# A hybrid attention/Hyena step: one adaLN chunk moved from TensorE to VectorE

## The chip, the cores and the metric

The kernel runs on one NeuronCore of one Trainium2 chip. The metric is device time in microseconds (us) of one execution. Five engines run in parallel on the core: TensorE (PE in the profile, its weight loads PEld), VectorE (DVE), ScalarE (ACT), GpSimd (POOL) and SyncE (SP, which here only issues DMAs). Each works through its own instructions in the order in which they were issued.

## The reference, cut to what matters

A two-layer diffusion backbone on 384 tokens (256 latent, 128 context), width 2048, everything in 32-bit floats. Per layer:

```python
shift, scale, gate = split(silu(c) @ w_ada[l] + b_ada[l], 3)     # adaLN: one vector for latents, one for context
h    = rmsnorm(x, norm_g) * (1 + scale) + shift
proj = h @ w_in                          # 2048 x 6144: q|k|v|g_att|hyena x0,x1,v|g_hy
att  = attend(q, k_all, v_all) * silu(g_att)
hy   = hyena(x0, x1, v) * silu(g_hy)     # short convolution, then a long one by Fourier transform
x    = x + gate * (concat(att, hy) @ w_out)
```

The adaLN part is a product of two vectors (one for the latents, one for the context) with a 2048 x 6144 matrix in each layer. Its output is cut into 12 chunks of 512 columns: chunks 0 to 3 are the shift, 4 to 7 the scale, 8 to 11 the gate. Chunk (1, 5) is a quarter of the scale of layer 1; it must be there when layer 1 forms its input h, at the end of layer 0.

## The kernel before, in words

The large products run as units. A unit is one 128 x 2048 block of weights, loaded in two halves of 512 KB into seven raw buffers `raw`. Each half is split into a high part `hi` (ACT, L225) and a rest `lo` (DVE, L231), and three matmuls (hi x hi, hi x lo, lo x hi; L831 to L833 or L803 to L805) give the product in nearly full precision. A half's raw buffer is free once its `lo` is made. One pass of the main loop is a step: it multiplies one unit on PE, splits halves of the next two units, evacuates the product and runs waiting background work (attention, the Fourier convolution). Layer 0 has, after a start phase, units of kind "b" (q, k, v; four steps each), 40 units "a" (f = 8 to 15 for x0; 16, 24, 17, 25, ... 23, 31 for x1 and v in turn; 0 to 7 and 32 to 39 for the two gates) and 16 units "o" (the output projection, f = 0 to 15). Layer 1 has the same.

The 16 adaLN chunks that are not needed at the start are spread over these steps. The string `HOW` says how each is made, in the order (0, 8), (0, 9), (0, 10), (0, 11), (1, 4), (1, 0), (1, 5), (1, 1), (1, 6), (1, 2), (1, 7), (1, 3), (1, 8) to (1, 11):

- "P", on PE (`ada_mm`, L283): four units of four small matmuls each (`adab`), then one copy by ACT, four transposes (L297), and two small DVE instructions. `P_0` says in which steps of layer 0 a unit is loaded; it is multiplied one step later, after the unit's matmuls.
- "D", on DVE (`ada_acc`, L357 and L359): 32 multiply-adds over 128 x 512, 16 for each of the two vectors, into two accumulators `pa0` and `pa1`. They wait in a queue `vq`; the lists `R_Q`, `R_X0`, `R_X1`, `R_G`, `R_O` (layer 0) and `R_1` say how many run in each step, at the step's end (`run_q`; up to two that could not run are owed to the next step). A finished chunk is added up over the partitions by PE in the next step (`ada_sum`, four matmuls, L379), copied by ACT (L381) and transposed in the step after that (`ada_fin2`, L387). The next chunk's first multiply-add stays queued until the sum has been issued.
- "G", the gap chunks (1, 3) and (1, 7): their weights are loaded during the output projection of layer 0 into the buffers that attention and convolution have left, and PE multiplies them around the layer boundary, where it waits for the norm. Their results are copied by ACT (L290) into the accumulator buffers `pa0` and `pa1`, of which there is one each (`PAB = 1`).

`load_ada` is called at the end of each step: it loads a unit of a "P" chunk if it is due, and then halves of "D" chunks while fewer multiply-adds are queued than the next two steps want and a raw buffer is free. All these loads go through the SP queue, in the order of the program.

At the layer boundary the last unit of the output projection (f = 15) is evacuated (L879), the norm's sums go over PE (L421), ACT and DVE, and back over PE (L435); ACT copies the result to `rs` (L436). Then `make_h` builds the input of layer 1: DVE scales (L446), ACT adds the shift and rounds (L450, `hh`), DVE takes the rest (L453, `hl`). The matmuls of layer 1 (L803 to L805) need `hh` and `hl`.

Of the kernel before, what the change touches and what calls it, by code (L numbers as in the profile page):

```python
# [29 lines left out]
HIB = 4  # L30
LOB = 3
PAB = 1
HOW = 'PDPDDDPDDDGGDDDD'
SQ = 3
MAINB = 4
AH = 2
# [4 lines left out]
EB = 0.8  # L41
W0, W1, W2, W3, W4 = 6, 8, 4, 24, 0
R_Q = [0, 0, 0, 0, 2, 2, 4, 5]
R_X0 = [5, 6] * 4
R_X1 = [5, 6] * 2 + [5] + [4, 4, 4, 3] + [2, 1, 0, 0, 1, 2, 2]
R_G = [2, 1, 1, 0, 0, 1, 3, 4, 4, 6, 6, 6, 6, 6, 5, 0]
R_O = [3] + [5] * 14 + [0]
R_1 = [0] * 12 + [4] * 21 + [1] * 14 + [6] * 5 + [0] * 20
P_0 = [1] * 6 + [0] * 19 + [1] * 6 + [0] * 33
GAP_L, GAP_P = (0, 1, 3, 7, 8, 9, 11, 12), (5, 6)  # L50
P_1 = [0] * 72
BUD = 2.0
# [18 lines left out]
def step_kernel(ctx, tc, xT, vec, cst, delta, zfeat, fw, ada, wb, wc, wo, ck, cv, qk1, yT, nk, nv):  # L71
# [75 lines left out]
    free = [one.tile([128, 1024], F32, name=f"raw{n}") for n in range(RAWB)]  # L147
# [10 lines left out]
    def fetch(u, h, of=None):  # L158
        u.raw[h] = free.pop(0)
        if of:  # L160
            u.of = of
            held[of] += 1
        nc.sync.dma_start(out=u.raw[h], in_=u.src[:, h * 1024:(h + 1) * 1024])
# [37 lines left out]
    def load_ada(n, p):  # L201

        state["pe"] += p
        if state["pe"] and by_pe and len(free) > 1:
            state["pe"] -= 1
            u = by_pe.pop(0)
            for h in range(2):
                fetch(u, h)
            on_pe.append(u)
        while by_dve and len(vq) < n and free:  # L210
            i, h = divmod(state["ada"], 2)
            u = by_dve[0]
            fetch(u, h)
            ada_acc(u, h)
            state["ada"] += 1
            if h == 1:
                by_dve.pop(0)
# [115 lines left out]
    vq, by_pe, by_dve, on_pe = [], [], [], []  # L333

    def ada_acc(u, h):
        l, ch, kc = u.kw["l"], u.kw["ch"], u.kw["kc"]
        if kc == 0 and h == 0:
            pacc[0] = {"left": 32}
        st = pacc[0]

        def done():
            st["left"] -= 1
            if st["left"] % 4 == 0:
                release(u, h)
            if st["left"] == 0:
                sums.append(lambda: ada_sum(l, ch, st))
                urgent.append((state["step"] + 1, run_sums))

        def op(t, v):
            if v not in st:  # L350
                st[v] = accs_p.tile([128, 512], F32, name=f"pa{v}", tag=f"pa{v}")
            acc = st[v]
            w = u.raw[h][:, t * 512:(t + 1) * 512]
            k = kc * 4 + 2 * h + t
            sc = scT[:, k, v:v + 1]
            if k == 0:
                nc.vector.tensor_scalar(acc, w, sc, None, ALU.mult)  # L357
            else:
                nc.vector.scalar_tensor_tensor(out=acc, in0=w, scalar=sc, in1=acc, op0=ALU.mult, op1=ALU.add)  # L359
            done()  # L360

        for t in range(2):
            for v in range(2):
                vq.append((kc + h + t + v == 0, lambda t=t, v=v: op(t, v)))
# [547 lines left out]
    def ada_units(l, ch, how="P"):  # L912
        return [Unit(ada[l, ch, kc], "ada", l=l, ch=ch, kc=kc, how=how) for kc in range(4)]
# [26 lines left out]
    chunks += [(1, ch) for ch in range(8, 12)]  # L940
    for (l, ch), how in zip(chunks, HOW):
        if how != "G":
# [6 lines left out]
    gap = ada_units(1, 3) + ada_units(1, 7)  # L949
    spare = [p[:, 1024 * i:1024 * (i + 1)] for p, n in ((P1, 3), (P2, 4), (P3, 3), (P4, 2)) for i in range(n)]  # L950
    mains = []
    for l in range(NL):
        us = ([k_unit(1, j) for j in range(4)] if l else []) + layer_units(l)

        for u, n, p in zip(us, R_1 if l else R_Q + R_X0 + R_X1 + R_G + R_O, P_1 if l else P_0):
            u.dq, u.pe = n, p
# [27 lines left out]
    with tc.manual_schedule():  # L984
# [18 lines left out]
        for i, u in enumerate(units + mains):  # L1003
# [28 lines left out]
            l = u.kw["l"]  # L1032
# [72 lines left out]
            if v is not None:  # L1105
                load_ada(v.dq + (v.nxt.dq if v.nxt is not None else 0), v.pe)
# [97 lines left out]
```

## Time and profile before

| | before |
|---|---|
| median of 3 runs | 1493.04 us (1490.0 to 1494.1) |
| the profiled execution: its time | 1492.46 us |
| its span, from first to last instruction | 1490.7 us |
| PE busy | 1461.4 us (98%) |
| DVE busy | 976.7 us (66%) |
| ACT busy | 586.2 us (39%) |
| mean DMA rate | 192 GB/s |
| mean granted PE clock | 0.994 |

Times in the profile's views are us from the start of the span. A row of a timeline gives start, duration, engine, line of the program, operation, output <- inputs, shapes and, in brackets, how long the engine was idle just before it and what ended that. Rows that follow each other closely are merged (x4). A matmul's stated duration includes its way through the array; the distance of the starts of two rows is the time that PE spent on the first. "x8" in a row of small matmuls counts four weight loads and four matmuls.

### The profile page before, as it was taken

The page shows a single profiled execution, that of the slowest core. Times are in us where ns is not written, and L with a number is a line of the kernel's source. Part 1 is how long each engine was busy: PE and PEld are TensorE (multiplying, and loading weights), DVE is VectorE, ACT ScalarE, POOL GpSimd, SP SyncE. Part 2 cuts the span into 40 slices and gives each one's busy share as a digit, 9 for nine tenths or more (in the row PEclk, how much of TensorE's full clock was granted, in tenths as well). Part 3 has the DMA queues.
Part 4 walks back from the last instruction along what each step waited for, and adds up shares of the span by engine and source line. Part 5 has one row for each costly group of instructions (what it writes and reads, how often), then busy time and mean ns, then how long its engine had stood idle before and what let it go on. Part 6 is the DMA issues. An engine that isn't in the chain of part 4 may idle for free.

```text
span 1490.7 us, 20718 instructions
## 1 busy us (share of the span) xinstructions
PE 1461.4 (98%) x8032; PEld 1293.2 (87%) x8032; DVE 976.7 (66%) x1619; ACT 586.2 (39%) x975; POOL 51.1 (3%) x94
## 2 busy tenths in 40 slices
PE   9999999999999999999999999999999999999995
PEld 5346777999998999999997888899999999999995
DVE  6734556777877566697687655766777756755443
ACT  2423554555432322343334545455433332244331
POOL 1110000000000000001110000000000000000001
PEclk9999999999999999999999999999999999999997
DMA  9999366444566543569894333543445343544422
GB/s 349 414 358 346 134 224 224 163 152 155 172 223 215 206 144 132 184 196 327 282 329 152 115 120 135 194 145 128 156 170 184 128 171 128 196 158 149 148 98 85
DMA packets 78731, 286.48 MB, mean 192 GB/s; under 512 B 9670, under 2 KB 10504, under 8 KB 78120
## 3 DMA queue, kind: packets, MB, share of 16 engines
q1 hardware_dynamic: 72824, 267.19, 50.8%
q0 software_dynamic: 5808, 17.97, 3.3%
q8 instruction: 63, 1.03, 0.3%
q14 instruction: 36, 0.29, 0.1%
HBM read 271.49 MB, written 13.63 MB: 191 GB/s over the span
## 4 chain that ended last, share of the span: by engine, by line
PE 91%; DMA 5%; DVE 2%; ACT 1%; issue 1%; SPq 0%; DVEq 0%; ACTq 0%
PE acc L831 21%; PE acc L833 21%; PE acc L832 21%; PE acc L803 6%; PE acc L805 6%; PE acc L804 6%; PE adab L283 2%; PE bgb L665 1%; PE bgb L648 1%; DMA hh1b<-in_ada 1%; DMA hl2b<-in_wb 1%; PE bgb L756 1%; DMA hl1b<-in_ada 1%; DMA XM<-in_xT 1%; PE bgb L658 1%; DMA raw<-in_wb 1%
## 5 line engine op out<-in xcount | busy, mean ns | idle before, releaser
L831 PE MATMUL acc<-hh,hi 128*128 128x384 f32 x1792 | 613.9, 343 | 0.0
L833 PE MATMUL acc<-hh,lo 128*128 128x384 f32 x1792 | 602.7, 336 | 0.0
L832 PE MATMUL acc<-hl,hi 128*128 128x384 f32 x1792 | 602.6, 336 | 0.0
L225 ACT CAST hi<-raw 128x1024 fp32r<-128x1024 f32 x282 | 294.4, 1045 | 318.0 <-issue 168.0
L231 DVE TENSOR_TENSOR lo<-raw,hi 128x1024 fp32r<-128x1024 f32 x282 | 343.0, 1219 | 116.3 <-issue 53.9
L831 PEld LDWEIGHTS acc<-hh,hi 128*128 128x128 f32 x1792 | 337.0, 188 | 12.5 <-issue 8.9
L832 PEld LDWEIGHTS acc<-hl,hi 128*128 128x128 f32 x1792 | 337.0, 188 | 3.7 <-issue 1.4
L833 PEld LDWEIGHTS acc<-hh,lo 128*128 128x128 f32 x1792 | 336.8, 188 | 0.0
L359 DVE SCALAR_TENSOR_TENSOR pa<-raw,scT,pa 128x512 f32<-128x512 f32 x330 | 225.9, 744 | 0.0
L803 PE MATMUL acc<-hi,hh 128*128 128x512 f32 x384 | 156.2, 407 | 4.2 <-ACT hh L450 3.9
L804 PE MATMUL acc<-lo,hh 128*128 128x512 f32 x384 | 152.2, 396 | 0.8 <-DVE lo L231 0.8
L805 PE MATMUL acc<-hi,hl 128*128 128x512 f32 x384 | 152.6, 397 | 0.0
L803 PEld LDWEIGHTS acc<-hi,hh 128*128 128x128 f32 x384 | 72.5, 189 | 37.4 <-issue 13.4
L805 PEld LDWEIGHTS acc<-hi,hl 128*128 128x128 f32 x384 | 72.5, 189 | 18.1 <-DVE hl L453 0.7
L804 PEld LDWEIGHTS acc<-lo,hh 128*128 128x128 f32 x384 | 72.6, 189 | 17.6 <-DVE lo L231 1.5
L406 ACT ACTIVATE tt<-XM 128x384 f32<-128x384 f32 x48 | 24.4, 523 | 135.2 <-DVE XM L879 131.0
L879 DVE SCALAR_TENSOR_TENSOR XM<-acc,mod,xo 128x256 f32<-128x256 f32 x64 | 23.7, 412 | 67.0 <-PE acc L833 67.0
L722 DVE SCALAR_TENSOR_TENSOR z<-acc,V,z 128x255 f32<-128x255 f32 (+1 forms) x64 | 25.2, 414 | 37.5 <-ACT z L718 36.4
L722 DVE SCALAR_TENSOR_TENSOR XM<-acc,V,XM 128x255 f32<-128x255 f32 (+1 forms) x64 | 25.2, 414 | 30.1 <-ACT XM L718 29.0
L283 PE MATMUL adab<-raw,scT 128*32 128x512 f32 x248 | 41.0, 610 | 2.7 <-ACT tt L406 1.5
L722 DVE SCALAR_TENSOR_TENSOR x1c<-acc,V,x1c 128x255 f32<-128x255 f32 (+1 forms) x64 | 25.2, 414 | 26.5 <-ACT x1c L718 25.3
L450 ACT ACTIVATE hh<-tt,mod 128x256 fp32r<-128x256 f32 x64 | 24.7, 446 | 37.5 <-DVE tt L446 37.5
(188 smaller groups left out, 1109.1 us busy)
## 6 DMA issues: line engine op xcount, KB each, us to landing
raw<-in_wc SPq DMA_DIRECT2D x160, 512.0 KB, 3.8
raw<-in_ada SPq DMA_DIRECT2D x150, 512.0 KB, 5.2
raw<-in_wo SPq DMA_DIRECT2D x64, 512.0 KB, 4.4
raw<-in_wb SPq DMA_DIRECT2D x58, 512.0 KB, 4.6
P<-in_ada SPq DMA_DIRECT2D x16, 512.0 KB, 8.0
Hd<-P POOLq DMA_DIRECT2D x24, 256.0 KB, 8.8
P<-Hd SPq DMA_DIRECT2D x4, 1536.0 KB, 8.6
XM<-in_xT SPq DMA_DIRECT2D x4, 768.0 KB, 11.4
```

Source lines behind the costliest of these rows:

```text
L225: nc.scalar.copy(u.hi[h], u.raw[h])
L231: nc.vector.tensor_tensor(u.lo[h], u.raw[h], u.hi[h].bitcast(F32), ALU.subtract)
L283: mm(part[32 * t:32 * t + 32, :], scT[:, kc * 4 + t, :], u.raw[t // 2][:, (t % 2) * 512:(t % 2 + 1) * 512], start=(kc == 0), stop=(kc == 3))
L359: nc.vector.scalar_tensor_tensor(out=acc, in0=w, scalar=sc, in1=acc, op0=ALU.mult, op1=ALU.add)
L450: nc.scalar.activation(hh[:, kt, a:b], t[:, a:b], AF.Identity, bias=mod[l][:, kt, v:v + 1])
L722: nc.vector.scalar_tensor_tensor(out=out[:, o:o + n], in0=bank[:, i:i + n], scalar=w(k), in1=out[:, o:o + n], op0=ALU.mult, op1=ALU.add)
L803: mm(accs[g][m], hh[:, kt, ms], wh[:, k, :], start=first, stop=False)
L804: mm(accs[g][m], hh[:, kt, ms], wl[:, k, :], start=False, stop=False)
L805: mm(accs[g][m], hl[:, kt, ms], wh[:, k, :], start=False, stop=last)
L831: mm(b[:, :T], wh, hh[:, kt, :], start=(kt == 0), stop=False)
L832: mm(b[:, :T], wh, hl[:, kt, :], start=False, stop=False)
L833: mm(b[:, :T], wl, hh[:, kt, :], start=False, stop=(kt == 15))
```

## The change

The seventh letter of `HOW`, chunk (1, 5), turns from P to D. The lists of multiply-adds are raised for it in layer 0, mostly from 5 to 6 per step, `P_0` now loads the eight remaining PE units in the first eight steps, and `load_ada` gets one more condition: no multiply-add of a gate chunk of layer 1 is loaded before the gap chunks are done.

```diff
-HOW = 'PDPDDDPDDDGGDDDD'
+HOW = 'PDPDDDDDDDGGDDDD'
...
-R_X0 = [5, 6] * 4
-R_X1 = [5, 6] * 2 + [5] + [4, 4, 4, 3] + [2, 1, 0, 0, 1, 2, 2]
-R_G = [2, 1, 1, 0, 0, 1, 3, 4, 4, 6, 6, 6, 6, 6, 5, 0]
-R_O = [3] + [5] * 14 + [0]
+R_X0 = [6] * 8
+R_X1 = [6] * 4 + [6] + [5, 5, 5, 5] + [4, 3, 2, 1, 1, 2, 2]
+R_G = [2, 2, 2, 1, 1, 2, 4, 5, 6, 6, 6, 6, 6, 6, 5, 0]
+R_O = [4] + [6] * 14 + [0]
...
-P_0 = [1] * 6 + [0] * 19 + [1] * 6 + [0] * 33
+P_0 = [1] * 8 + [0] * 56
...
-        while by_dve and len(vq) < n and free:
+        while by_dve and len(vq) < n and free and (gap == [] or by_dve[0].kw["ch"] < 8 or by_dve[0].kw["l"] == 0):
```

## The prediction, made before the changed kernel was built or run

> **What bounds the kernel now.** I read the page first: engines and the chain that ended last.
>
> ```profile
> span 1490.7 us, 20718 instructions
> PE 1461.4 (98%) x8032; PEld 1293.2 (87%) x8032; DVE 976.7 (66%) x1619; ACT 586.2 (39%) x975; POOL 51.1 (3%) x94
> PE 91%; DMA 5%; DVE 2%; ACT 1%; issue 1%; SPq 0%; DVEq 0%; ACTq 0%
> ```
>
> PE is busy nearly always, and 91% of the chain is PE. A busy share is a mean over stages, so I then asked for the stretch that the change touches, layer 0 from its first "a" unit to its last "o" unit. Columns: stretch, length, busy time of PE, PEld, DVE, ACT, POOL with instruction counts, granted PE clock, DMA share, GB/s.
>
> ```profile
> 256.00:794.00 538.00, 538.00 (x3127) 512.70 (x3125) 395.26 (x628) 198.67 (x312) 17.36 (x32) 1.00 0.60 206
> ```
>
> PE has no idle microsecond in these 538 us. Here every piece of PE work taken out shortens the time by its own length, and work on DVE costs nothing until PE has to wait for it. DVE is busy 73% of the stretch.
>
> Third, the layer boundary, where PE does wait: timelines of ACT, DVE and PE.
>
> ```profile
> 801.96 0.59 ACT L290 COPY pa<-adab 128x512 f32<-128x512 f32 x1 [4.76 <-PE bgb L379]
> 802.44 0.48 ACT L436 COPY acc<-bgb 128x384 f32<-128x384 f32 x1
> 802.81 1.06 ACT L225 CAST hi<-raw 128x1024 fp32r<-128x1024 f32 x1
> 804.02 0.82 ACT L450 ACTIVATE hh<-tt,mod 128x256 fp32r<-128x256 f32 x2
> ...
> 802.96 0.74 DVE L446 SCALAR_TENSOR_TENSOR tt<-XM,asc,bgb 128x256 f32<-128x256 f32 x2 [3.71 <-ACT acc L436]
> ...
> 797.88 0.91 PE L435 MATMUL bgb<-tt,ones 128*128 128x128 f32 x6
> 798.71 2.78 PE L283 MATMUL adab<-P,scT 128*32 128x512 f32 x24
> 801.31 0.61 PE L379 MATMUL bgb<-pa,ones 128*32 128x256 f32 x8
> 801.74 1.04 PE L283 MATMUL adab<-P,scT 128*32 128x512 f32 x8
> 804.60 0.50 PE L803 MATMUL acc<-hi,hh 128*128 128x512 f32 x1 [1.82 <-ACT hh L450]
> 806.32 0.80 PE L803 MATMUL acc<-hi,hh 128*128 128x512 f32 x1 [0.70 <-ACT hh L450]
> 815.62 0.60 PE L297 MATMUL bgb<-C,pa 128*128 128x128 f32 x4
> 816.19 0.48 PE L803 MATMUL acc<-hi,hh 128*128 128x512 f32 x1
> 824.67 0.60 PE L297 MATMUL bgb<-C,pa 128*128 128x128 f32 x4
> ```
>
> Read it backwards. PE waits at 804.60 for `hh` (ACT L450). ACT is late because it sat idle 4.76 us before its copy L290 into `pa`: with one `pa0`, the gap chunk's result must wait until the sum of the last DVE chunk, (1, 2), has read it, and that sum (L379) stands on PE only at 801.31, behind 2.60 us of gap products. The norm copy L436 could have run when L435 ended at 798.71, but it is queued behind L290; DVE's L446 waits for L436, and everything of layer 1 for that.
>
> **The change, part by part.** First, PE work that goes. The six PE units that stand in steps f = 28, 21, 29, 22, 30, 23, from the chain (start, us, what; x8 is four weight loads and four matmuls), the work around them, and the restart behind them:
>
> ```profile
> 444.75 0.99 PE adab L283 x8
> ...
> 464.79 1.56 PE adab L283 x8
> ...
> 499.01 1.00 PE adab L283 x8
> ...
> 440.55 0.57 PE bgb L379 x8
> ...
> 454.46 0.38 PE L387 MATMUL bgb<-C,tt 128*128 128x128 f32 x2
> 454.77 1.06 PE L283 MATMUL adab<-raw,scT 128*32 128x512 f32 x8
> ...
> 464.19 0.60 PE L297 MATMUL bgb<-C,tt 128*128 128x128 f32 x4
> 464.72 1.63 PE L283 MATMUL adab<-raw,scT 128*32 128x512 f32 x8
> ...
> 445.67 0.45 PE L831 MATMUL acc<-hh,hi 128*128 128x384 f32 x1
> 445.96 0.34 PE L832 MATMUL acc<-hl,hi 128*128 128x384 f32 x1
> 446.14 0.34 PE L833 MATMUL acc<-hh,lo 128*128 128x384 f32 x1
> ```
>
> A unit costs PE about 1.0 us, not four times the 0.6 us of one matmul: the four run side by side. Five units are 0.99 to 1.00, one 1.56; in all 6.5 us. Four of these six are chunk (1, 5); two are the end of (0, 10), which with `P_0 = [1] * 8` come at the end of the "b" units instead: 2.0 us come back there. One set of L297 transposes goes: 464.19 to 464.72, 0.53 us. In their place stands one more sum (L379, 0.57) with its L387 (0.31 by the starts). Moreover the sum of (1, 2) moves from the boundary into a step, another 0.88 there. Each new interruption of a unit's run costs a restart: 0.29 us to the second matmul instead of 0.17 to 0.18, 0.1 us; I count three more. Sum: -6.5 + 2.0 - 0.53 + 2 x 0.88 + 0.3 = -3.0 us. Bounds: -2.4, if the 1.56 was a stall that comes back elsewhere, to -3.6.
>
> Second, the boundary. Does (1, 2) end earlier? Stepping `run_q` and `load_ada` through the lists by hand: before, 224 multiply-adds (seven chunks) are needed in layer 0; 153 have run by the end of step f = 39, and the remaining 71 go 3, 4, 6, five times 5, 1, 7, five times 5: the last runs at f = 14, so its sum falls behind f = 15, where the row at 801.31 shows it. After, 256 are needed; 183 have run by f = 39 and the remaining 73 go 4, 5, 7, 6, 6, 6, 6, 1, 8, 6, 6, 6, 6: the last runs at f = 12, the sum at f = 13, L387 at f = 14. The new condition in `load_ada` keeps the next chunk from taking `pa0` and `pa1`. So L290 finds `pa0` free. Then: L435 ends at 798.7, L436 takes 0.48 (to 799.3; L290, 0.59, is done before), L225 0.95 more (800.2), L450 starts then, and PE may start 0.58 later (804.02 to 804.60), at 800.8. PE itself is through with its gap products at 801.31 + 1.0 = 802.3 without the 0.43 of L379. So PE is late next, not `hh`: it starts at 802.3 instead of 804.6, 2.3 us earlier. The second block of `hh`, 2.30 after the first L450 (806.32), comes at 802.5, before PE needs it at 803.0; its wait goes too. The first unit of layer 1 takes 804.60 to 815.62, 11.0 us; the next 816.19 to 824.67, 8.5. The 2.5 between them is that second wait (0.7 by its row, with the pieces around it about 1) and this:
>
> ```profile
> 806.30:809.50 3.20, 3.18 (x8) 2.53 (x9) 3.20 (x10) 2.22 (x6) 0.00 (x0) 0.50 0.00 0
> ```
>
> The granted clock (third from the end) falls to 0.50 after the two waits: eight matmuls take 3.2 us, against 0.235 each otherwise: 1.4 us lost. Without the waits I take the clock to stay at 1.00, as in the rows before them. Boundary: -2.3 - 2.5 = -4.8 us. Bounds: -0.4 (only L379 gone, ACT waits for something else) and -4.8 (no wait left); I take -4.8, as 4.76 us of wait have one named cause.
>
> The Trainium skill, page "TensorE: Matmul & The Clock Gate", Part 1, says the clock halves after an idle window of about 3.4 us. The gaps here are 1.8 and 0.7 us; by that rule the slow stretch need not come from them and could stay, and the time would be about 1486.5.
>
> Third, DVE. 32 more multiply-adds:
>
> ```profile
> 642.26 4.05 DVE L359 SCALAR_TENSOR_TENSOR pa<-raw,scT,pa 128x512 f32<-128x512 f32 x6
> ...
> 785.95 0.74 DVE L879 SCALAR_TENSOR_TENSOR XM<-acc,mod,xo 128x256 f32<-128x256 f32 x2 [0.84 <-PE acc L833]
> ...
> 788.89 3.39 DVE L359 SCALAR_TENSOR_TENSOR pa<-raw,scT,pa 128x512 f32<-128x512 f32 x5
> ...
> 794.27 0.74 DVE L879 SCALAR_TENSOR_TENSOR XM<-acc,mod,xo 128x256 f32<-128x256 f32 x2 [0.85 <-PE acc L833]
> ```
>
> Six take 4.05 us, so 0.68 each, 22 us in all, hidden by DVE's idle time. In the output projection a step is 8.32 us (785.95 to 794.27); with 5 DVE idles 0.85 of it, with 6 it keeps 0.17: nearly full, not over. The step that runs 8 falls 0.6 behind. What is queued behind the multiply-adds is the `lo` of a later unit's second half, which PE reads half a unit (4.2 us) after the next evacuation; lateness under 4 us is covered. Tightest are the steps of the Fourier products, where PE's step shrinks too. The DVE rows that open them:
>
> ```profile
> 465.09 1.65 DVE L722 SCALAR_TENSOR_TENSOR z<-acc,V,z 128x255 f32<-128x255 f32 x4 [1.50 <-ACT z L718]
> ...
> 475.66 1.64 DVE L722 SCALAR_TENSOR_TENSOR x1c<-acc,V,x1c 128x255 f32<-128x255 f32 x4 [2.16 <-ACT x1c L718]
> ...
> 487.26 1.65 DVE L722 SCALAR_TENSOR_TENSOR z<-acc,V,z 128x255 f32<-128x255 f32 x4 [3.65 <-ACT z L718]
> ```
>
> At f = 21: two more multiply-adds (+1.35), a PE step shorter by 1.3, 0.35 of small DVE work moved away, 1.50 idle: 0.8 us late. At f = 29: 0.8 + 1.35 + 2.1 - 0.35 - 2.16 = 1.7 late. At f = 22 the idle time takes it back. 1.7 is under 4: nothing. Without that cover PE would pay those 1.7.
>
> Loads: bytes stay the same; they move earlier on SP's queue. In the output projection:
>
> ```profile
> raw<-in_ada SPq DMA_DIRECT2D x17, 512.0 KB, 6.2
> DMA to landing us min/median/max: 3.6/5.8/12.1
> ```
>
> A half loaded in one step is used in the next at the earliest, a step (8.4 us) later; the median landing is 6.2. Main loads queue on SP behind an adaLN load that waits for a buffer; its release comes at most one multiply-add later than before, 0.7 us. ACT loses an L290 and gains an L381: nothing. POOL is not touched.
>
> Sum: -3.0 - 4.8 = -7.8 us. The profiled execution took 1492.46, 1.76 more than its span: 1482.9 + 1.8 = 1484.7. The median of the runs is 0.6 above that execution; I say 1485.
>
> **Rivals.**
> (a) The clock stays at half behind the boundary: 1486.5. Against it, the slow stretch begins right behind the waits.
> (b) ACT's copy waits for something else, and the boundary keeps its stall: 1485 + 4.4 = 1489.4, no change that can be told. For it: L290 has only been seen late; against it, the profile names only L379.
> (c) DVE's lateness in the Fourier steps reaches PE: 1487 to 1489.
> (d) Slower: adaLN halves land late in the output projection. With six per step, about eight of its 18 halves have only one step of lead. If they landed in 12.1, the longest seen, DVE would wait 8 x 3.7 = 30 us; 2 are taken by idle time, 4 by PE's half unit: 1485 + 24 = 1509. It turns the gain into a loss from waits of 14 us on, a landing of about 10 us. Against it: the median of 6.2, and no wait of DVE for a load in the list of waits of this stretch.
>
> **How the numbers follow.** The forecast has 0.60, (a) 0.13, (b) 0.12, (c) 0.08, (d) 0.07. A change under 0.3%, 4.5 us, can't be told from none; 1488.5 divides. Faster: 0.60 + 0.13 and a quarter of (c), less a little for the spread of a median of three: 0.74. Same: (b), the rest of (c) and that spread: 0.19. Slower: 0.07. The range leaves out (d) and the far ends: 1481.5 (the largest of each term, and 2 us of spread) to 1490 (rival b).
>
> **What would show it.** Right: L283 absent between 440 and 500; L379 of (1, 2) a step before the end of the output projection; ACT's L290 at about 798 without a wait; PE's first L803 of layer 1 about 2 us behind L435's gap products with clock 1.00; PE without idle in layer 0. Wrong: PE waiting for `lo` (L833, L805) or DVE for a load in the output projection, or L290 still waiting.

## The result and the profile after

The changed kernel takes 1482.96 us in the median of 6 runs (1482.08 to 1485.08), the kernel before 1493.04 (1490.0 to 1494.1): ratio 0.994, 95% interval 0.993 to 0.995. In two later sets of runs it was 0.9947 (0.9934 to 0.9959) and 0.9944 (0.9931 to 0.9956). The forecast was 1485.0. The page after:

```profile
span 1480.5 us, 20711 instructions
PE 1452.9 (98%) x8006; PEld 1289.3 (87%) x8006; DVE 996.9 (67%) x1651; ACT 585.8 (40%) x975; POOL 51.1 (3%) x94
PE 94%; DMA 2%; DVE 2%; ACT 1%; issue 1%; SPq 0%; DVEq 0%; ACTq 0%
```

The rows answer to those shown of before: PE has 26 matmuls and 8.5 us of work less, DVE 32 instructions and 20.2 us more (0.63 each), and the span fell by 10.2 us, more than PE's busy time. PE still carries the chain.

Where the 10.2 us lie is read from three starts on PE that both kernels have: the first PE unit of the "b" steps (L283), the L283 ahead of the norm's L421, and the first transposes of layer 1 (L297). Before, from the timeline of PE:

```profile
186.27 1.06 PE L283 MATMUL adab<-raw,scT 128*32 128x512 f32 x8
...
794.16 1.06 PE L283 MATMUL adab<-P,scT 128*32 128x512 f32 x8
```

After (before's L297 stands in the prediction, at 815.62):

```profile
185.01 1.06 PE L283 MATMUL adab<-raw,scT 128*32 128x512 f32 x8
...
788.95 1.06 PE L283 MATMUL adab<-P,scT 128*32 128x512 f32 x8
...
805.64 0.60 PE L297 MATMUL bgb<-C,pa 128*128 128x128 f32 x4
```

First to second mark ("the steps"): 607.89 before, 603.94 after, -3.95. Second to third ("the boundary"): 21.46 before, 16.69 after, -4.77. From there to the end of the span: 675.08 and 674.86, 0.22 apart. The rest, 1.26, lies ahead of the first mark, where the change touches nothing. That mark stood between 185.0 and 188.3 in the profiled executions of this study, 185.01, 187.62 and 185.47 in the three of the changed kernel, while its steps were 603.94 in all three. So the change is worth 8.7 us between these two traces, and single executions differ by some 3 us more in the start phase. (The last section shows that 1.45 of the 8.7 depend on the execution too.) In the table, which later sections use, each number is a difference of two such starts in the trace of that run:

| run | steps | boundary |
|---|---|---|
| before | 607.89 | 21.46 |
| after, as_changed, as_changed_b | 603.94 | 16.68 to 16.69 |
| early_sum | 608.86 | 16.68 |
| late_sum | 602.93 | 21.50 |
| early_p2 | 607.92 | 20.01 |
| p_fourier | 606.50 | 16.68 |
| fourier7 | 607.29 | 16.69 |
| o8 | 611.23 | 16.68 |
| two_chunks | 601.26 | 18.58 |
| two_chunks_b | 601.32 | 16.68 |
| two_chunks_c | 599.64 | 16.68 |

The boundary after, timelines of ACT, DVE and PE:

```profile
792.84 0.58 ACT L290 COPY pa<-adab 128x512 f32<-128x512 f32 x1 [0.79 <-PE adab L283]
793.67 0.48 ACT L436 COPY acc<-bgb 128x384 f32<-128x384 f32 x1 [0.25 <-PE bgb L435]
...
794.99 0.80 ACT L450 ACTIVATE hh<-tt,mod 128x256 fp32r<-128x256 f32 x2
...
794.18 0.74 DVE L446 SCALAR_TENSOR_TENSOR tt<-XM,asc,bgb 128x256 f32<-128x256 f32 x2
...
771.30 0.64 PE L379 MATMUL bgb<-pa,ones 128*32 128x256 f32 x8
...
793.56 3.64 PE L283 MATMUL adab<-P,scT 128*32 128x512 f32 x32
797.13 0.50 PE L803 MATMUL acc<-hi,hh 128*128 128x512 f32 x1
```

The last sum, L379 of chunk (1, 2), stands at 771.30, two steps ahead of the end. L290 waits for its own product only and L436 follows when L435 is done. `hh` is begun at 794.99, before PE is through with its gap products. PE's first L803 has no bracket: PE did not wait.

The windows around it, with the whole stretch first (columns as in the prediction; the granted clock is third from the end):

```profile
257.00:790.00 533.00, 533.00 (x3109) 511.80 (x3101) 415.95 (x664) 198.41 (x314) 17.34 (x32) 1.00 0.59 208
788.95:797.13 8.18, 8.04 (x67) 3.48 (x66) 4.87 (x13) 3.91 (x9) 1.09 (x2) 1.00 0.32 107
797.13:800.00 2.87, 2.87 (x16) 2.37 (x13) 2.75 (x9) 1.95 (x7) 0.00 (x0) 1.00 0.04 16
```

PE is busy in all 533 us, and the clock stays at 1.00 behind the boundary.

### The profile page after: what moved, and what is told of

Same layout as the page of the kernel before. It is cut to its first block, busy times and chain, and to the rows that moved or that the text cites. A ratio compares the mean times of both kernels' runs of the same rounds, so it can differ in the third digit from the quotient of the medians.

```text
span 1480.5 us, 20711 instructions
## 1 busy us (share of the span) xinstructions
PE 1452.9 (98%) x8006; PEld 1289.3 (87%) x8006; DVE 996.9 (67%) x1651; ACT 585.8 (40%) x975; POOL 51.1 (3%) x94
## 4 chain that ended last, share of the span: by engine, by line
PE 94%; DMA 2%; DVE 2%; ACT 1%; issue 1%; SPq 0%; DVEq 0%; ACTq 0%
PE acc L831 21%; PE acc L833 21%; PE acc L832 21%; PE acc L803 6%; PE acc L805 6%; PE acc L804 6%; PE adab L283 2%; PE bgb L665 1%; PE bgb L648 1%; DMA hh1b<-in_ada 1%; PE bgb L756 1%; PE bgb L658 1%; DMA raw<-in_wb 1%; PE bgb L566 1%; PE bgb L524 1%
## 5 line engine op out<-in xcount | busy, mean ns | idle before, releaser
L359 DVE SCALAR_TENSOR_TENSOR pa<-raw,scT,pa 128x512 f32<-128x512 f32 x360 | 246.0, 745 | 0.3 <-DMA raw<-in_ada 0.3
L803 PE MATMUL acc<-hi,hh 128*128 128x512 f32 x384 | 155.3, 404 | 1.7 <-ACT hh L450 1.4
L803 PEld LDWEIGHTS acc<-hi,hh 128*128 128x128 f32 x384 | 72.1, 188 | 35.3 <-issue 15.1
L283 PE MATMUL adab<-raw,scT 128*32 128x512 f32 x216 | 35.0, 604 | 4.6 <-DMA raw<-in_ada 4.6
```

The source lines that it names most:

```text
L283: mm(part[32 * t:32 * t + 32, :], scT[:, kc * 4 + t, :], u.raw[t // 2][:, (t % 2) * 512:(t % 2 + 1) * 512], start=(kc == 0), stop=(kc == 3))
L803: mm(accs[g][m], hh[:, kt, ms], wh[:, k, :], start=first, stop=False)
```

## The experiments

Kernels that are compared share the runs of before, whose medians were 1491.96 for as_changed, early_sum, late_sum and two_chunks, 1493.18 for two_chunks_b, o8, p_fourier and fourier7, 1491.97 for as_changed_b and two_chunks_c, 1492.49 for early_p2.

**as_changed**: the changed kernel again, no edit.

> The changed kernel once more, in the same rounds as the three others, as their yardstick. The two traces put the gain at -3.95 us in the steps of layer 0 (from the first "a" unit's predecessor at 184 to the end of the output projection), -4.77 us at the layer boundary, and -1.26 us before 185 us, where the change touches nothing. If the last part is the spread of the start phase, the medians should differ by about 8.7 us here (ratio 0.9942); if it belongs to the change, by 10.0 us (0.9933).

1484.02 us (1483.1 to 1485.01), ratio 0.9947 (0.9934 to 0.9959), 7.9 below before. Steps and boundary are those of the first trace to 0.01; the start phase is 2.6 later. The first run's extra microsecond or two belongs to that spread.

**early_sum**: the boundary's part alone. The six PE units stay where they were; the last multiply-adds of (1, 2) run earlier, and the gate chunks wait for the gap chunks.

```diff
-R_O = [3] + [5] * 14 + [0]
+R_O = [4] + [6] * 14 + [0]
...
-        while by_dve and len(vq) < n and free:
+        while by_dve and len(vq) < n and free and (gap == [] or by_dve[0].kw["ch"] < 8 or by_dve[0].kw["l"] == 0):
```

> The boundary alone. The kernel before, chunk (1, 5) still on PE; only R_O is [4] + [6] * 14 + [0] and the gate chunks wait for the gap chunks, so that the last multiply-add of (1, 2) runs at f = 12 and its sum at f = 13. Theory (the boundary stall is ACT's copy L290 waiting for the sum that has to empty pa0): L290 waits no more than for its own product, the first L803 of layer 1 follows the gap products without idle PE, the granted clock behind it is 1.00, and the time falls by 4.8 us less 0.2 for two restarts: 1488.4. Rival (the boundary gain came with the PE work that left, not with the sum's place): L290 as late as before, no gain, 1493.

1488.1 us (1486.75 to 1490.31, 11 runs), ratio 0.9974 (0.9965 to 0.9982): -3.9 against before in the same runs. The expectation had counted -4.6. In the trace the boundary is 16.68, 4.78 shorter as expected, but the steps are 0.97 longer: the sum and its L387 moved into them, and only 0.2 had been counted for that. ACT's copy in early_sum's timeline, and its window behind the boundary:

```profile
799.34 0.58 ACT L290 COPY pa<-adab 128x512 f32<-128x512 f32 x1 [0.79 <-PE adab L283]
```

```profile
803.60:806.00 2.40, 2.40 (x14) 1.97 (x11) 2.25 (x7) 1.48 (x5) 0.00 (x0) 1.00 0.02 9
```

With all the PE work still there and the sum two steps earlier, the 4.76 us wait is gone, and PE starts the first unit of layer 1 at full clock.

**late_sum**: the change, with its last multiply-adds as late as before.

```diff
-R_O = [4] + [6] * 14 + [0]
+R_O = [4] + [5] * 14 + [0]
```

> The PE work alone. The changed kernel with R_O = [4] + [5] * 14 + [0]: the last multiply-add of (1, 2) runs at f = 14 again and its sum falls behind f = 15. Theory: L290 waits about 4.8 us for L379 again, PE idles about 1.8 us and 0.7 us, the clock is 0.50 for about 3 us behind that, and the time is that of the changed kernel plus 4.6. Rival of the Trainium skill's page "TensorE: Matmul & The Clock Gate", Part 1 (an idle window of about 3.4 us is needed for the half clock): the waits come back, but the clock stays at 1.00, plus 3.2. Rival (the boundary gain has another cause): as the changed kernel.

1488.31 us (1485.94 to 1491.62, 11 runs), ratio 0.9975 (0.9966 to 0.9984): 4.3 above as_changed, where 4.6 had been expected. The boundary is 21.50 again, the steps 1.01 shorter, which is the sum leaving them. Timelines of ACT and PE, and two windows, of late_sum:

```profile
798.31 0.58 ACT L290 COPY pa<-adab 128x512 f32<-128x512 f32 x1 [4.76 <-PE bgb L379]
...
800.95 0.50 PE L803 MATMUL acc<-hi,hh 128*128 128x512 f32 x1 [1.82 <-ACT hh L450]
802.67 0.51 PE L803 MATMUL acc<-hi,hh 128*128 128x512 f32 x1 [0.70 <-ACT hh L450]
```

```profile
799.61:803.02 3.41, 1.37 (x5) 0.78 (x5) 2.21 (x7) 2.38 (x6) 0.00 (x0) 1.00 0.00 1
803.02:806.43 3.41, 3.41 (x10) 2.57 (x9) 3.41 (x12) 1.96 (x5) 0.00 (x0) 0.50 0.00 0
```

The wait of 4.76 is back to the digit, with it PE's two waits, and the slow clock behind them (0.50 for 3.41 us). late_sum has the new condition in `load_ada` and keeps the stall, so the condition alone does not remove it. These two runs show the boundary's part from both sides: it comes from the place of one sum. They also split the gain. By the traces the move of the sum alone is worth 3.8 us (-4.78 + 0.97, early_sum), the PE work alone 4.9 (-4.96 + 0.04, late_sum against before); by the medians 3.9 and 3.7.

**p_fourier**: two of the eight remaining PE units go back into the steps of the Fourier products, f = 28 and f = 21.

```diff
-P_0 = [1] * 8 + [0] * 56
+P_0 = [1] * 6 + [0] * 19 + [1] * 2 + [0] * 37
```

> The changed kernel with two of its eight remaining PE units taken from the end of the b units and put where units stood before the change, behind the Fourier products of f = 28 and f = 21. Theory (a unit there costs PE more than its 1.0: the run from the Fourier product's matmuls to the unit's start is longer by 0.5 to 0.6, which the prediction's count of the unit's own duration left out): the run L756 to the next piece is about 3.6 in front of the unit instead of 3.0, and the steps take about 1.0 longer than 603.9, 604.5 to 605.2. Rival (a unit costs the same wherever it stands, and the 0.95 us by which the steps gained more than forecast come from elsewhere): 603.9 within 0.2, and 3.0 in front of the unit.

1486.19 us in one run; the steps are 606.50, +2.56, more than either side expected. PE's timeline of p_fourier:

```profile
379.79 0.44 PE L831 MATMUL acc<-hh,hi 128*128 128x384 f32 x1 [0.42 <-ACT P L729]
...
442.40 3.59 PE L756 MATMUL bgb<-P,C 128*128 128x512 f32 x8
446.66 1.05 PE L283 MATMUL adab<-raw,scT 128*32 128x512 f32 x4 [0.67 <-DMA raw<-in_ada]
447.95 1.05 PE L283 MATMUL adab<-raw,scT 128*32 128x512 f32 x4 [0.24 <-DMA raw<-in_ada]
```

1.33 of the 2.56 are these three waits, two for late loads of the unit and one 60 us ahead of it. Of the other 1.23, 0.56 stand where the theory puts them: from L756 to PE's next work it is 3.59 without the wait, 3.03 in the changed kernel. But a load was late at the same place, and only one of the two units stands behind L756, so the run by itself does not decide between the two sides. The rest is not traced to rows.

**early_p2**: so the reverse was tried on the kernel before, all six units moved out of the Fourier steps and nothing taken away.

```diff
-R_G = [2, 1, 1, 0, 0, 1, 3, 4, 4, 6, 6, 6, 6, 6, 5, 0]
+R_G = [2, 1, 1, 1, 1, 1, 3, 4, 4, 6, 6, 6, 6, 6, 5, 0]
...
-P_0 = [1] * 6 + [0] * 19 + [1] * 6 + [0] * 33
+P_0 = [1] * 12 + [0] * 52
```

> The kernel before with its last six PE units moved from the Fourier steps into the six steps right behind the first six, at the end of the b units and in the first x0 steps (one multiply-add each added at f = 3 and f = 4 of the gate units, so that the queue empties in time). Nothing is taken from PE: the same units, transposes and sums as before. Theory (a unit behind a Fourier product costs PE more than elsewhere, by 0.6 behind L756 and 0.5 behind L748, and the one of 1.56 was a stall): the steps take about 1 less than before's 607.89, 606.5 to 607.1, the boundary stays at 21.5, the time is 1 below before, ratio 0.9993. Rival (a unit costs the same everywhere; the 0.95 by which the change's steps beat the forecast lie elsewhere): 607.9 within 0.2. Against both: DVE's multiply-adds in the x0 steps get later loads, and PE waits: over 608.

A first version, early_p, with `R_G` at 2 in its first six steps, was a program that deadlocks and has no time. early_p2 took 1491.99 us (1490.84 to 1494.65, 10 runs), ratio 1.0 (0.999 to 1.0009), steps 607.92: the theory that the Fourier steps are dearer falls. Its pieces were right: summed over the steps, the distances from the start of L756 to the next piece fall by 0.59, L748's by 0.51, L283's own by 0.55 (the stall of 1.56 is gone). But the same units now stand behind attention's L648, and there they cost as much: the eight runs of L648 go from 7.98 to 9.54 us. One of them in PE's timeline of before, then one with its unit in that of early_p2:

```profile
264.69 1.45 PE L648 MATMUL bgb<-P,P 128*128 128x384 f32 x4
```

```profile
269.11 1.46 PE L648 MATMUL bgb<-P,P 128*128 128x384 f32 x4
270.49 1.07 PE L283 MATMUL adab<-raw,scT 128*32 128x512 f32 x8
```

In front of a unit's matmul L648 keeps PE for 1.38 to 1.39 us, nearly its whole stated 1.46; in the row of before the next piece, a main matmul, starts 1.00 after it, at 265.69. So a unit costs its own 1.0 and a piece of what stands ahead of it: 0.5 to 0.6 behind L756 and L748, 0.39 behind L648, 0.17 behind L566 at the end of the "b" steps. That is most of what taking units out saved beyond their own length. (The boundary of this run, 20.01, is taken up in the last section.)

**fourier7**: more multiply-adds in two Fourier steps, to see where DVE's lateness reaches PE.

```diff
-R_X1 = [6] * 4 + [6] + [5, 5, 5, 5] + [4, 3, 2, 1, 1, 2, 2]
-R_G = [2, 2, 2, 1, 1, 2, 4, 5, 6, 6, 6, 6, 6, 6, 5, 0]
+R_X1 = [6] * 4 + [6] + [5, 5, 5, 5] + [4, 7, 7, 1, 0, 0, 0]
+R_G = [0, 0, 1, 1, 2, 2, 4, 5, 6, 6, 6, 6, 6, 6, 5, 0]
```

> The changed kernel with 7 multiply-adds each in the Fourier steps f = 21 and f = 29 instead of 3 and 2, and fewer in the next ones. DVE then opens f = 29's evacuation about 3.5 us late and f = 22's about 7.8 late. Theory (PE's cover is half a unit, about 4 us): no wait of PE at f = 29, but one for lo of about 3.5 us in f = 22 or f = 30, and the steps take 607 to 608 instead of 603.9. Rival (the lateness is taken up by buffers): no wait of PE, 603.9 within 0.5.

1485.52 us in one run, steps 607.29, +3.35: the theory's size, but not made up as it said. DVE and PE of fourier7:

```profile
467.90 1.64 DVE L722 SCALAR_TENSOR_TENSOR z<-acc,V,z 128x255 f32<-128x255 f32 x4
...
479.43 1.22 DVE L231 TENSOR_TENSOR lo<-raw,hi 128x1024 fp32r<-128x1024 f32 x1
480.56 1.64 DVE L722 SCALAR_TENSOR_TENSOR x1c<-acc,V,x1c 128x255 f32<-128x255 f32 x4
...
480.70 0.44 PE L833 MATMUL acc<-hh,lo 128*128 128x384 f32 x1 [2.00 <-DVE lo L231]
...
494.33 0.49 PE L779 MATMUL bgb<-C,P 128*128 128x128 f32 x2 [0.65 <-DVE P L770]
```

ACT's L718, which DVE's evacuation follows, ends at 464.30 for f = 29 and at 472.88 for f = 22. So DVE opens them 3.6 and 7.7 us late, as expected. At the first PE does not wait; behind the second it waits 2.00 for the `lo` made just ahead of that evacuation. Half a unit of cover would have made it 3.5. The cover measured here is 5.7 us, as PE has more than half a unit to do there: a Fourier product (L748, 1.32 us) comes first. A smaller wait (0.65) follows at an operand of the inverse Fourier product, which was not forecast, and 0.7 of the 3.35 are not traced to rows. That the total came out as forecast is in part luck.

**o8**: DVE made late in the output projection.

```diff
-R_G = [2, 2, 2, 1, 1, 2, 4, 5, 6, 6, 6, 6, 6, 6, 5, 0]
-R_O = [4] + [6] * 14 + [0]
+R_G = [2, 2, 2, 1, 1, 2, 4, 5, 2, 2, 2, 2, 2, 2, 2, 0]
+R_O = [8] * 14 + [0] * 2
```

> The changed kernel with multiply-adds held back in the gate units and 8 instead of 6 per step of the output projection, 100 in its steps f = 0 to 12. At 0.68 each beside some 3.45 of other DVE work per step, DVE needs about 113 us for steps in which PE needs 101: it ends about 12 late. Theory of the prediction (DVE's lateness costs nothing up to the half unit, 4.2 us, by which PE needs lo later, and everything beyond it): PE waits for lo (L833's operand) in the later of these steps, about 8 us in all, the time is the changed kernel's + 8, about 1492. Rival without cover: + 12, and PE waits from the first full step. Rival that DVE's lateness never reaches PE (deeper buffers): + 0.

1490.5 us (1488.83 to 1491.89, 10 runs), ratio 0.9984 (0.9975 to 0.9993); steps +7.29. The size is the theory's, the place is not. PE's waits in o8's timeline, and a window behind the longest:

```profile
703.89 0.98 PE L379 MATMUL bgb<-pa,ones 128*32 128x256 f32 x6 [1.63 <-DVE pa L359]
...
741.11 1.20 PE L379 MATMUL bgb<-pa,ones 128*32 128x256 f32 x8 [0.26 <-DVE pa L359]
...
778.53 1.64 PE L379 MATMUL bgb<-pa,ones 128*32 128x256 f32 x8 [2.25 <-DVE pa L359]
```

```profile
778.50:781.90 3.40, 3.37 (x14) 2.20 (x15) 2.81 (x5) 1.03 (x2) 0.77 (x2) 0.50 0.99 354
```

PE never waits for `lo` here. It waits 4.1 us in all for the last multiply-add of a finished chunk, whose sum stands at a fixed place in PE's queue and has no half unit of cover; and behind the longest wait the clock is half for 3.4 us, 1.7 us lost; the last 1.4 of the 7.29 I trace to no row. So a cover of half a unit or more stands behind `lo` (fourier7), and none behind the sums.

**two_chunks**: chunk (0, 10) to DVE as well.

```diff
-HOW = 'PDPDDDDDDDGGDDDD'
-R_Q = [0, 0, 0, 0, 2, 2, 4, 5]
-R_X0 = [6] * 8
-R_X1 = [6] * 4 + [6] + [5, 5, 5, 5] + [4, 3, 2, 1, 1, 2, 2]
-R_G = [2, 2, 2, 1, 1, 2, 4, 5, 6, 6, 6, 6, 6, 6, 5, 0]
-P_0 = [1] * 8 + [0] * 56
+HOW = 'PDDDDDDDDDGGDDDD'
+R_Q = [0, 0, 0, 2, 4, 4, 4, 6]
+R_X0 = [7] * 8
+R_X1 = [7] * 5 + [6, 5, 5, 5] + [4, 3, 2, 1, 1, 2, 2]
+R_G = [2, 2, 2, 1, 1, 2, 4, 6, 8, 8, 8, 8, 8, 7, 5, 0]
+P_0 = [1] * 4 + [0] * 60
```

> A candidate: (0, 10) goes to DVE as well. HOW = PDDDDDDDDDGGDDDD, 288 multiply-adds in layer 0 instead of 256: R_Q starts a little earlier, R_X0 and the first of R_X1 run 7, the later gates 8; P_0 keeps the four units of (0, 8). The last sum still falls before f = 15. Theory (PE is the bound, DVE work is free while its lateness stays under half a unit): four units of 1.0 us and 0.43 of transposes go, one sum (0.57), its transposes (0.2) and restarts (0.2) come: -3.5 us against the changed kernel, about 1479.5. Rival (DVE or the raw buffers are the bound now: a step of a late gate unit with 8 multiply-adds needs about 8.25 of its 8.36 us): PE waits for lo or DVE for loads, no gain or a loss.

1483.26 us (1482.58 to 1484.29), ratio 0.9942 (0.9929 to 0.9956), 0.8 below as_changed instead of 3.5: a miss. The steps gained 2.7, the boundary lost 1.9. DVE and PE of two_chunks:

```profile
796.52 0.23 DVE L390 TENSOR_TENSOR mod<-bgb,V 128x4 f32<-128x4 f32 x2 [2.65 <-PE bgb L387]
...
797.73 0.50 PE L803 MATMUL acc<-hi,hh 128*128 128x512 f32 x1 [0.26 <-ACT hh L450]
799.44 0.50 PE L803 MATMUL acc<-hi,hh 128*128 128x512 f32 x1 [0.70 <-ACT hh L450]
```

Its last multiply-add ran at f = 13, one step too late: the chunk's L387 then stood at the boundary, behind gap products, and DVE's L390 and all of `hh` waited for it.

**two_chunks_b**: the same chunk, with lists that end at f = 12 in place of those of two_chunks.

```diff
+R_Q = [0, 0, 0, 2, 4, 4, 4, 5]
+R_X0 = [5, 6] + [7] * 6
+R_X1 = [7] * 5 + [6, 6, 6, 6] + [4, 3, 2, 1, 1, 2, 2]
+R_G = [2, 2, 2, 2, 2, 2, 4, 7, 8, 8, 8, 8, 8, 8, 6, 2]
+R_O = [6] + [6] * 14 + [0]
```

> The second chunk on DVE once more, with lists that run its multiply-adds earlier: the last one at f = 12 of the output projection, its sum at f = 13, L387 at f = 14, so none of it stands at the boundary. Theory (each P unit taken from PE pays as in the first change as long as DVE has idle time, and the boundary is free while the last sum is in a step): the steps take 600.6 us instead of 603.9 (four units of 1.0 and a set of transposes of 0.53 less, a sum and its L387 of 0.88 more, 0.3 for restarts), the boundary from the first of L421's sums to the first transposes of layer 1 stays at 16.7, the time is 3.3 below the changed kernel's on this chip: about 1480.7, ratio 0.992. Rival: DVE is full in these steps (two_chunks lost about 1.1 us in the first x0 steps), and what PE saves it waits for: the steps stay at 602.5 to 604, the time within 1.5 of the changed kernel's.

1482.17 us (1481.33 to 1482.93), ratio 0.9932 (0.992 to 0.9945). The boundary is 16.68, as expected; the steps gained 2.6 of 3.3. One wait of PE more than accounts for the missing 0.7:

```profile
648.24 7.11 DVE L458 TENSOR_TENSOR hl<-XM,hh 128x384 fp32r<-128x384 f32 x15
...
658.80 0.44 PE L832 MATMUL acc<-hl,hi 128*128 128x384 f32 x1 [1.61 <-DVE hl L458]
```

DVE, with 8 multiply-adds a step, was late at the 16 small L458 that make the output projection's input. Without this wait the steps would have gained about 4.3, so the forecast of 3.3 was short here too.

**as_changed_b** (no edit) and **two_chunks_c** (two_chunks_b with the gate steps' list spread):

```diff
-R_G = [2, 2, 2, 2, 2, 2, 4, 7, 8, 8, 8, 8, 8, 8, 6, 2]
+R_G = [2, 3, 3, 4, 4, 5, 6, 7, 8, 7, 7, 7, 7, 6, 4, 1]
```

> The changed kernel once more, as the yardstick for the next two on the same chip: 0.994 of before, about 1483.5.

> two_chunks_b with the multiply-adds of the gate units spread otherwise: up to 7 in the early ones, where DVE idled 1 to 3.5 us a step, and 7, 6, 4, 1 instead of 8, 8, 6, 2 in the last, ahead of DVE's 16 small L458 (7.1 us), for which PE waited 1.6 us in two_chunks_b. The last multiply-add stays at f = 12. Theory (two_chunks_b fell short of its forecast by that one wait): PE does not wait for L458, the steps take 1.7 less than two_chunks_b's 601.32, 599.6, the boundary stays at 16.7, the time is about 4 below the changed kernel's on this chip, ratio to before 0.9915. Rival: DVE is full over the whole stretch, and the wait moves to another lo or sum: steps 601 to 601.5.

as_changed_b: 1483.13 us (1483.06 to 1484.86), ratio 0.9944 (0.9931 to 0.9956). two_chunks_c: 1478.7 us (1477.77 to 1480.62), ratio 0.9913 (0.9898 to 0.9928), faster than both kernels of this study; steps 599.64 of 599.6 expected. On its trace PE waits for no L458; in the stretch of the steps it is busy all but 0.14 us, in its window:

```profile
256.00:790.00 534.00, 533.86 (x3119) 511.41 (x3119) 431.73 (x694) 198.23 (x315) 17.93 (x33) 1.00 0.62 213
```

DVE is busy 81% of the stretch, against 78% after the change (415.95 of 533) and 73% before: where the multiply-adds stand in the steps decided what they cost.

## Why the prediction was right, and where a size was off

*PE work.* Forecast -3.0 (bounds -2.4 to -3.6), measured -3.95, outside these bounds. The terms by the traces, each the sum of start-to-start distances over the steps: L283 -4.53 (forecast -6.5 + 2.0), L297 -0.53 (forecast the same). A sum with its L387 and the restarts costs 0.97 in early_sum and 1.01 in late_sum, so two cost 2.0; forecast 1.76 and 0.3. What is left is -0.9. The term that was mis-sized is the cost of a unit, taken as "Five units are 0.99 to 1.00, one 1.56": the row's own duration. L756 and L748 shortened by 0.60 and 0.50 besides, as no unit stands behind them any more; L566, with a unit more behind it, grew by 0.18. The same rows, which the prediction read for L283 alone, hold it: before, L756 at 441.05 to L283 at 444.68 is 3.63.

*The boundary.* Forecast -4.8, measured -4.77, by the path forecast: L290 waits no more, PE is late next instead of `hh`, the second wait and the slow clock go. early_sum and late_sum show that the sum's place alone does it. PE starts 8.18 us behind the second mark, 10.44 before: 2.26 earlier, forecast 2.3; the unit's run falls from 11.02 to 8.51. That the full 4.8 came is in part luck: the prediction read the slow clock's 1.4 us from one execution of before, and early_p2, with the same two waits, does not have it (last section).

*DVE.* DVE rows of the changed kernel:

```profile
464.94 1.64 DVE L722 SCALAR_TENSOR_TENSOR z<-acc,V,z 128x255 f32<-128x255 f32 x4
...
474.28 1.64 DVE L722 SCALAR_TENSOR_TENSOR x1c<-acc,V,x1c 128x255 f32<-128x255 f32 x4
...
482.73 1.64 DVE L722 SCALAR_TENSOR_TENSOR z<-acc,V,z 128x255 f32<-128x255 f32 x4 [0.28 <-ACT z L718]
...
766.04 4.06 DVE L359 SCALAR_TENSOR_TENSOR pa<-raw,scT,pa 128x512 f32<-128x512 f32 x6
771.41 0.74 DVE L879 SCALAR_TENSOR_TENSOR XM<-acc,mod,xo 128x256 f32<-128x256 f32 x2 [0.18 <-PE acc L833]
```

The first two have no bracket, where before they had 1.50 and 2.16: DVE is late there, and the third has idle time again. ACT's L718 ended at 463.99 and 472.30 ahead of them, so DVE is 0.95 and 1.98 late; the forecast was 0.8 and 1.7. In the output projection 0.18 of idle time is left, forecast 0.17. PE waits for none of it. For `lo` the prediction's cover of 4.2 us was too small rather than too large (5.7 in fourier7). That a chunk's sum has none, it did not see; o8 shows it.

*Loads.* Rival (d) needed late adaLN halves. The group of multiply-adds on the page after:

```profile
L359 DVE SCALAR_TENSOR_TENSOR pa<-raw,scT,pa 128x512 f32<-128x512 f32 x360 | 246.0, 745 | 0.3 <-DMA raw<-in_ada 0.3
```

All 360 of them waited 0.3 us in all for loads. Rival (b) is refuted by early_sum, rival (c) by PE's 533 busy microseconds of 533. Rival (a) said that the slow clock could stay without the waits: it did not in any trace with a boundary of 16.7, where the first unit of layer 1 runs 8.50 to 8.51 us, nor in two_chunks with its smaller gaps.

*The total.* 1484.7 was summed for an execution like the profiled one; the profiled one after took 1482.53. Of the 2.2 between them 0.95 are the steps' size and 1.26 the start phase of that execution.

## What to carry to other kernels

When the result of one engine must be read by a second before a third may write, look for where that reader stands in its queue: here one matmul group of 0.6 us, moved by two steps, was worth nearly as much as the chunk of work that was moved off TensorE (3.8 and 4.9 us by the traces). On TensorE here, a piece's price was the difference of its neighbours' starts with and without it (1.2 to 1.6 us for a unit), not its own duration (1.0). Background work that fits by the average fits only if each step ahead of a fixed reader (a sum, a batch of rounding, the last step before a stage) has room: the same multiply-adds were worth 0.8 us or 4.4 us by their place.

## What the runs showed of the hardware that was not expected

The clock's drop is not tied to the gaps alone. early_p2 left the boundary as it was and shows the same two waits of PE, to the digit, and no slow clock:

```profile
806.06 0.50 PE L803 MATMUL acc<-hi,hh 128*128 128x512 f32 x1 [1.82 <-ACT hh L450]
807.77 0.51 PE L803 MATMUL acc<-hi,hh 128*128 128x512 f32 x1 [0.70 <-ACT hh L450]
```

So behind the same gaps the granted clock was 0.50 (before, late_sum) and 1.00 (early_p2), and the boundary took 21.5, 21.5 and 20.0 us: 1.45 of the boundary's 4.8 are paid in some executions only.

What decides it can be read from the traces. Each trace records when the granted clock changed. In all thirteen, the recorded changes lie whole multiples of 3.413 us apart, and every slow stretch before the last stage lasts 3.41 us at 0.50. So the clock changed only on a grid of 3.413 us, which lies differently in each execution. The windows on that grid, before and then early_p2:

```profile
802.78:806.19 3.41, 1.02 (x4) 0.48 (x3) 2.14 (x6) 2.49 (x7) 0.00 (x0) 1.00 0.00 0
806.19:809.60 3.41, 3.28 (x8) 2.63 (x9) 3.30 (x10) 2.33 (x7) 0.00 (x0) 0.50 0.00 0
...
803.05:806.46 3.41, 1.59 (x18) 0.49 (x10) 1.16 (x4) 2.88 (x6) 0.00 (x0) 1.00 0.14 58
806.46:809.87 3.41, 2.71 (x12) 1.79 (x11) 3.09 (x11) 1.74 (x5) 0.00 (x0) 1.00 0.00 0
```

Before, both gaps fall into one stretch of the grid: PE idles 2.39 of 3.41 us, and the next stretch is slow. In early_p2 an edge of the grid, at 806.46, stands between the gaps: 1.82 idle in one stretch, 0.70 in the next, and the clock stays. The other waits fit. PE idled 2.04 in the stretch ahead of the slow one in late_sum and 2.21 in o8. The wait of 2.00 in fourier7 is cut by an edge at 479.87 into 1.17 and 0.83, that of two_chunks_b leaves 1.61 in one stretch, and neither lowered the clock. Over all stretches of the grid in the thirteen traces, from the first record of the clock to 1450 us, the seven with 1.92 us or more of idle PE were each followed by a slow one, none with 1.78 or less was, and of the three with 1.82 to 1.84 one was. Five of these eight slow stretches lie in the first 56 us. In the last stage, behind 1450 us, smaller idle times were followed by half clock (1.23 in two_chunks_c), so idle time is not the whole measure.

An estimate from the two gaps of before: shifted along the grid, they leave 1.92 us or more in one stretch for 1.1 of the 3.41 us of possible places, and 1.82 or more for 2.3. So between one execution in three and two in three pays the 1.45. No run set the place of the grid.

The Trainium skill, page "TensorE: Matmul & The Clock Gate", Part 1, says that the activity is watched in a free-running window of about 3.4 us, so that the place of the work in the window counts; the grid of 3.413 us agrees with that. Its table, which puts the half clock behind an idle window of about 3.4 us, does not fit these traces: a stretch with 2.04 us of idle PE, of 3.41, was enough in late_sum, and no single gap ahead of the slow stretches at the boundary and in o8 was longer than 2.25 us.
